# A SwiGLU trunk in float32 halves: seven products of halves moved from the down to the up projection

## The chip, the cores and the metric

The kernel runs on one core of one Trainium2 chip. The metric is the device time of one execution in microseconds; the time before is the median of three runs, 2036.55 us (2036.38 to 2037.76).

## The reference

Two layers over a sequence of 512 tokens of width 1024, in float32. Each layer is SwiGLU, mixer (mLSTM in the first, sparse attention "NSA" in the second), SwiGLU; between the layers a shared K/V set is made. The four SwiGLUs are what the change rewrites:

```python
def rmsnorm(x, g):
    y = xf * lax.rsqrt(jnp.mean(xf * xf, axis=-1, keepdims=True) + EPS)
    return (y * g.astype(jnp.float32)).astype(x.dtype)

def swiglu(h, w_in, w_out):                 # w_in: 1024 x 5632, w_out: 2816 x 1024
    a, b = jnp.split(h @ w_in, 2, axis=-1)
    return (jax.nn.silu(a) * b) @ w_out
...
        h = h + 0.5 * swiglu(rmsnorm(h, ffn_norm[layer, 0]), ffn_w_in[layer, 0], ffn_w_out[layer, 0])
```

## The kernel before, in words

The stages run in the order ffn0, mLSTM, ffn1, K/V, ffn2, NSA, ffn3. The stream `h` lies transposed: eight tiles of 128 features x 512 tokens. A float32 product is made of three passes: each operand is split into a high part (rounded, written by ACT) and a low part (the rest, written by DVE), and `mm3` issues high x high, high x low and low x high. So one "strip" (a 128x128 block of weights times a 128x512 block of the stream) is three matmuls on PE, each with its own weight load (PEld).

A SwiGLU (`ffn`) goes through its 22 column blocks of 128 in pieces (`EVENS`: 8, 8, 6). For each block p it makes the gate block (columns p) and the up block (columns 22 + p), 8 strips each; DVE multiplies both by the row of 1/rms (`r`), ACT applies silu, DVE multiplies them and the result is split. After each piece the down projection adds to `h`: four pairs of output blocks, each 2n strips for a piece of n blocks.

In ffn 0, 1 and 3 (`SEVEN`) some pairs of down blocks (`PAIRS`, five of twelve) are made by Strassen's seven products of a 2x2 product instead of eight: the weights of the pair are quartered (`fetch`: q11, q12, q21, q22), DVE makes four sums of them (`add_quarters`: s1 to s4), the seven resulting forms are split like weights (`load_forms`, four groups: two, two, two and one form), and the gated values are halved along the tokens, with their own three sums (`gate_forms`). `down_seven` then runs seven products of 128x256 (`product`), into the halves of four PSUM banks X, Y, Z, V, and combines them on ACT and DVE.

Weights are loaded by `load_weight` in the order in which they are asked for; `weight` keeps two entries ready beyond the one in use, in three buffers of high and low parts (`whi`, `wlo`, 1024 columns: one whole block of weights, or one group of forms). The entry two ahead can so be split only when PE is done with the one before the current. Every engine works its own instructions in a fixed order, which the compiler's scheduler sets.

Of the kernel before, what the change touches and what calls it, by code (L numbers as in the profile page):

```python
# [96 lines left out]
class Net:  # L97
# [76 lines left out]
    def add_quarters(self, i, m, k0, n):

        q = self.raws[i, m, k0]
        s = self.sums[i, m, k0] = [None] + [self.fp.tile([P, 512], F32, name=f"s{j}", tag=f"s{j}", bufs=1)[:, :n * P]
                                            for j in range(1, 5)]
        self.nc.vector.tensor_tensor(s[1], q[2, 1], q[2, 2], op=ALU.add)
        self.nc.vector.tensor_tensor(s[3], q[1, 1], q[2, 1], op=ALU.subtract)  # L180
        self.nc.vector.tensor_tensor(s[2], s[1], q[1, 1], op=ALU.subtract)
        self.nc.vector.tensor_tensor(s[4], q[1, 2], s[2], op=ALU.subtract)

    def load_forms(self, i, m, k0, n, group):

        q, s = self.raws[i, m, k0], self.sums[i, m, k0]
        forms = ((q[1, 1], s[2]), (s[1], s[3]), (s[4], q[1, 2]), (q[2, 2],))[group]
# [3 lines left out]
        for j, f in enumerate(forms):  # L191
            c = slice(512 * j, 512 * j + n * P)
# [35 lines left out]
    def setup(self):  # L228
# [7 lines left out]
        for b in range(KB):  # L236
# [5 lines left out]
            if b == 1 and self.order:  # L242
                self.load_weight()
# [11 lines left out]
    def norm_in(self, gcol, ssq=True, loaded=False):  # L255
# [82 lines left out]
    def ffn(self, i, r=None):  # L338
# [4 lines left out]
        with ExitStack() as ctx:  # L343
# [23 lines left out]
            def gate_forms(pa, pb):  # L367


                fl = lambda t: t.rearrange("p f n -> p (f n)")  # L370
                if not half:
                    t = gp.tile([P, 3 * N], F32, name="ft", tag="ft", bufs=2)
                    gated(t[:, :T], pa, pb)
                    TT(t[:, T:], t[:, :N], t[:, N:T], op=ALU.subtract)
                    hi = gp.tile([P, 8, N], F32R, name="fhi", tag="fhi", bufs=4)
                    lo = gp.tile([P, 8, N], F32R, name="flo", tag="flo", bufs=4)
                    self.split(t, fl(hi[:, :3]), fl(lo[:, :3]))
                    gs.append((hi, lo))
                    half.append(t)
                    return  # L380
                one, (hi, lo) = half.pop(), gs[-1]
                t = gp.tile([P, 5 * N], F32, name="fv", tag="fv", bufs=1)
                gated(t[:, :T], pa, pb)
                self.split(t[:, :T], fl(hi[:, 3:5]), fl(lo[:, 3:5]))
                c = [t[:, N * j:N * j + N] for j in range(5)]
# [71 lines left out]
            for k0, k1 in EVENS if seven else THIRDS:  # L457
                gs, late, half = [], [], []
                n = k1 - k0
                for p in range(k0, k1):  # L460
# [3 lines left out]
                    if p == 0:  # L464
                        order.sort(key=lambda o: o[0] + 1.5 * o[1])
# [859 lines left out]
```

## Time and profile before

| | before |
|---|---|
| median of 3 runs | 2036.55 us |
| the profiled execution, own time | 2037.12 us |
| its span, first to last instruction | 2035.3 us |
| PE busy | 2020.1 us, 99% |
| DVE busy | 1298.4 us, 64% |
| ACT busy | 885.7 us, 44% |
| granted TensorE clock, mean | 1.000 |

The span is the time from the first to the last instruction of the profiled execution; its own time has 1.8 us more around it. PE's busy time overlaps from one matmul to the next (a record of 0.39 us, starts 0.23 us apart), so what a matmul costs is the distance between two starts. The same holds for DVE, whose records overlap by some 0.08 us.

### The profile page before, as it was taken

To read this page: it belongs to the slowest core of one execution; us is meant where nothing else is said; L and a number is where in the kernel's file an instruction comes from. 1 tells how busy PE (TensorE), PEld (TensorE's weight loads), DVE (VectorE), ACT (ScalarE), POOL (GpSimd) and SP (SyncE) were. 2 spreads that over 40 slices of the span, in tenths; PEclk is the share of its full clock that TensorE was granted. 3 is DMA by queue.
4 is the path that set the end of the run, shared out by engine and by line. 5 is a ranking of instruction groups with operands and counts; after the bars stand their busy time and mean duration, and the time that the engine had idled before them with its cause. 6 is when DMAs were issued, how large, how long until landed. Compare 5 with 4: busy or idle time off the path is not lost.

```text
span 2035.3 us, 26085 instructions
## 1 busy us (share of the span) xinstructions
PE 2020.1 (99%) x10007; PEld 1677.1 (82%) x10007; DVE 1298.4 (64%) x2192; ACT 885.7 (44%) x1533; POOL 163.7 (8%) x216
## 2 busy tenths in 40 slices
PE   9999999999999999999999999999999999999999
PEld 7888888788778888888888888888777788888887
DVE  7565656767786655657656444445778885565654
ACT  5333334445743333334443322224889863333332
POOL 0000000012200000000101000001444410000000
PEclk9999999999999999999999999999999999999999
DMA  5333322323223333322333333323111123233232
GB/s 189 98 99 94 95 91 68 117 83 94 63 99 103 89 108 94 88 94 88 99 116 115 115 93 93 104 89 102 52 43 43 42 80 102 78 118 94 74 111 80
DMA packets 61084, 188.22 MB, mean 92 GB/s; under 512 B 7328, under 2 KB 9760, under 8 KB 60960
## 3 DMA queue, kind: packets, MB, share of 16 engines
q1 hardware_dynamic: 59568, 183.82, 29.3%
q8 instruction: 78, 1.28, 0.3%
q10 hardware_dynamic: 1008, 1.70, 0.2%
q0 software_dynamic: 384, 1.05, 0.2%
q14 instruction: 46, 0.38, 0.1%
HBM read 177.10 MB, written 2.10 MB: 88 GB/s over the span
## 4 chain that ended last, share of the span: by engine, by line
PE 92%; DVE 3%; ACT 3%; DMA 1%; issue 1%; POOL 0%; SPq 0%; DVEq 0%; ACTq 0%
PE pmm L215 82%; PE S L215 3%; PE po L215 2%; PE vps L215 1%; PE pt L1094 1%; PE paux L215 1%; ACT pr L1062 1%; PE pn L215 1%; DVE wlo L158 1%; ACT whi L157 0%; ACT pth L224 0%; PE pt L215 0%; PE dm L215 0%; DMA q<-in_ffn_out 0%; DMA wraw<-in_ffn_in 0%
## 5 line engine op out<-in xcount | busy, mean ns | idle before, releaser
L215 PE MATMUL pmm<-xhi,whi 128*128 128x512 f32 x1672 | 656.6, 393 | 0.7 <-ACT whi L157 0.5
L215 PE MATMUL pmm<-xhi,wlo 128*128 128x512 f32 x1672 | 652.8, 391 | 0.2
L215 PE MATMUL pmm<-xlo,whi 128*128 128x512 f32 x1672 | 652.3, 390 | 0.6 <-DVE xlo L268 0.6
L157 ACT ACTIVATE whi<-wraw 128x1024 fp32r<-128x1024 f32 (+5 forms) x368 | 329.7, 908 | 640.7 <-PE pmm L215 510.8
L158 DVE TENSOR_TENSOR wlo<-wraw,whi 128x1024 fp32r<-128x1024 f32 (+5 forms) x368 | 386.0, 1057 | 75.2 <-ACT whi L157 73.0
L215 PEld LDWEIGHTS pmm<-xhi,wlo 128*128 128x128 f32 x1672 | 313.4, 187 | 66.7 <-DVE wlo L158 1.1
L215 PEld LDWEIGHTS pmm<-xhi,whi 128*128 128x128 f32 x1672 | 313.7, 188 | 63.6 <-ACT whi L157 1.0
L215 PEld LDWEIGHTS pmm<-xlo,whi 128*128 128x128 f32 x1672 | 313.6, 188 | 62.7 <-DVE xlo L268 1.4
L215 PE MATMUL pmm<-fhi,whi 128*128 128x256 f32 (+1 forms) x699 | 230.9, 330 | 0.0
L215 PE MATMUL pmm<-flo,whi 128*128 128x256 f32 (+1 forms) x699 | 229.0, 329 | 0.0
L215 PE MATMUL pmm<-fhi,wlo 128*128 128x256 f32 (+1 forms) x699 | 228.8, 328 | 0.0
L356 DVE TENSOR_TENSOR fu<-pmm,r 128x512 f32<-128x512 f32 x88 | 60.8, 691 | 252.3 <-PE pmm L215 252.3
L215 PEld LDWEIGHTS pmm<-fhi,whi 128*128 128x128 f32 x699 | 132.7, 190 | 14.8 <-ACT fw L435 2.8
L215 PEld LDWEIGHTS pmm<-flo,whi 128*128 128x128 f32 x699 | 132.7, 190 | 11.9
L215 PEld LDWEIGHTS pmm<-fhi,wlo 128*128 128x128 f32 x699 | 132.6, 190 | 11.8
L415 DVE SCALAR_TENSOR_TENSOR h<-pmm,h 128x512 f32<-128x512 f32 (+1 forms) x67 | 45.5, 682 | 116.4 <-PE pmm L215 116.4
L278 POOL TENSOR_TENSOR ssq<-ssq,sq 128x512 f32<-128x512 f32 x18 | 26.5, 1470 | 1038.2 <-ACT sq L277 1006.0
L1067 POOL TENSOR_SCALAR pr<-pr,rz,gate 128x512 f32<-128x512 f32 (+3 forms) x128 | 81.8, 645 | 108.7 <-DVE rz L1063 92.9
L224 ACT ACTIVATE fhi<-fv 128x512 fp32r<-128x512 f32 x66 | 48.8, 740 | 84.2 <-DVE fv L388 61.0
L1062 ACT ACTIVATE pr<-S,nx,c 128x512 f32<-128x512 f32 (+3 forms) x128 | 78.1, 615 | 6.7 <-PE pt L1094 5.6
L354 DVE TENSOR_TENSOR ft<-pmm,r 128x512 f32<-128x512 f32 x55 | 37.9, 688 | 57.2 <-PE pmm L215 50.9
L224 ACT ACTIVATE whi<-s 128x512 fp32r<-128x512 f32 (+1 forms) x60 | 33.8, 601 | 89.9 <-PE pmm L215 63.7
(341 smaller groups left out, 2762.2 us busy)
## 6 DMA issues: line engine op xcount, KB each, us to landing
wraw<-in_ffn_in SPq DMA_DIRECT2D x175, 512.0 KB, 3.5
wraw<-in_ffn_out SPq DMA_DIRECT2D x32, 512.0 KB, 3.6
q<-in_ffn_out SPq DMA_DIRECT2D x48, 256.0 KB, 2.8
wraw<-in_ffn_out SPq DMA_DIRECT2D x16, 448.0 KB, 3.3
wraw<-in_ffn_out SPq DMA_DIRECT2D x18, 384.0 KB, 3.2
wraw<-in_m_qk SPq DMA_DIRECT2D x8, 512.0 KB, 3.5
wraw<-in_m_v SPq DMA_DIRECT2D x8, 512.0 KB, 3.6
wraw<-in_m_og SPq DMA_DIRECT2D x8, 512.0 KB, 3.5
```

The lines of the kernel that those rows point to most:

```text
L157: nc.scalar.activation(hi[:p, c], raw[:p, c], AF.Copy)
L158: nc.vector.tensor_tensor(lo[:p, c], raw[:p, c], hi[:p, c].bitcast(F32), op=ALU.subtract)
L215: self.nc.tensor.matmul(out, lhsT, rhs, start=start, stop=stop)
L224: self.nc.scalar.activation(hi, src, AF.Copy)
L278: (nc.gpsimd if b < 4 else nc.vector).tensor_tensor(t, t, sq, op=ALU.add)
L354: TT(t, pa, r, op=ALU.mult)
L356: TT(u, pb, r, op=ALU.mult)
L415: STT(h[:, c], po[j][:, c], 0.5, h[:, c], op0=ALU.mult, op1=ALU.add)
L1062: nc.scalar.activation(s, S[:, i, :n], AF.Exp, bias=nx[:, i:i + 1], scale=cc, accum_out=z[:, i:i + 1])
L1067: nc.gpsimd.tensor_scalar(s, s, rz[:, i:i + 1], gate[:, tb, gi:gi + 1], op0=ALU.mult, op1=ALU.mult)
L1094: nc.tensor.transpose(pt[:, col:col + P], pr[br][:, ROW[tb] + sb * P:ROW[tb] + sb * P + P], self.ident)
```

## The change

In ffn 0, 1 and 3 no down block is made by seven products any more. Instead, `by_seven` makes pairs of up blocks by seven products of halves: all pairs but the first (blocks 0 and 1), ten a SwiGLU. For the pairs 4, 10, 14 and 20 (`GATES`) the gate blocks are made that way too, four more. Here the 2x2 cut is over two column blocks, the two halves of the 1024 input features and the two halves of the tokens. The forms of the stream are made once a SwiGLU, behind `norm_in` (`x_forms`: four sums of each pair of stream tiles, split into `thi` and `tlo`), while the two plain pairs of the first two blocks run. A raw quarter has two buffers (before one).

The up value is not multiplied by 1/rms any more, in all four SwiGLUs; `gate_plain` takes it straight from PSUM. The factor goes onto the down result: instead of one DVE instruction (h += 0.5 * po) there are two (d = 0.5 * po * r; h += d). The first block's strips are ordered with the up block 3.5 strips behind the gate block (before 1.5), and the second weight of the kernel is fetched after four of the eight tiles of x (before after two). In the mLSTM, `sigmoids` (a table load and four activations on ACT) is called inside `finish`, behind its Square, instead of ahead of `finish`.

```diff
-PAIRS = {0: (1, 3), 8: (1, 3), 16: (1,)}
+GATES = (4, 10, 14, 20)
...
+            def x_forms(k):
+                one, two = (gp.tile([P, 3 * N], F32, name="fw", tag="fw", bufs=2) for _ in range(2))
+                h2, c = self.h[k + 4], [two[:, N * j:N * j + N] for j in range(3)]
+                nc.scalar.activation(one[:, :T], self.h[k], AF.Copy, scale=g1)
+                TT(one[:, T:], one[:, N:T], one[:, :N], op=ALU.subtract)
+                STT(c[0], h2[:, N:], g2, one[:, T:], op0=ALU.mult, op1=ALU.subtract)
+                STT(c[1], h2[:, N:], g2, one[:, N:T], op0=ALU.mult, op1=ALU.subtract)
+                STT(c[2], h2[:, :N], g2, c[0], op0=ALU.mult, op1=ALU.subtract)
...
+                self.split(one[:, T:], hi[:, :N], lo[:, :N])
+                self.split(two, hi[:, N:], lo[:, N:])
...
+            def by_seven(p):
...
+                upcoming("fetch", p)
+                a11, s1 = self.weight("form", i, p, 0)
+                yield from product(X[:, :N], a11, 0)
+                nc.scalar.activation(W[:, 0, :], X[:, :N], AF.Copy)
+                yield from product(Y[:, :N], s1, -1)
+                s2, s3 = self.weight("form", i, p, 1)
+                yield from product(X[:, N:], s2, -2)
+                TT(U, X[:, N:], W[:, 0, :], op=ALU.add)
+                yield from product(Y[:, N:], s3, -3)
+                TT(W[:, 1:, :], U[:, None, :].to_broadcast([P, 2, N]), two(Y), op=ALU.add)
+                TT(u2[:, N:], W[:, 2, :], Y[:, :N], op=ALU.add)
+                s4, a12 = self.weight("form", i, p, 2)
+                yield from product(Z[:, N:], s4, 3)
+                yield from product(Z[:, :N], a12, 2)
+                TT(two(u1), W[:, :2, :], two(Z), op=ALU.add)
+                a22 = self.weight("form", i, p, 3)[0]
+                upcoming("add", p)
+                yield from product(V[:, :N], a22, -4)
+                TT(u2[:, :N], W[:, 2, :], V[:, :N], op=ALU.add)
+                return u1, u2
...
-                        STT(h[:, c], po[j][:, c], 0.5, h[:, c], op0=ALU.mult, op1=ALU.add)
...
+                            STT(d[:, c], po[j][:, c], 0.5, r[:, c], op0=ALU.mult, op1=ALU.mult)
+                            TT(h[:, c], h[:, c], d[:, c], op=ALU.add)
...
                 nc.scalar.activation(dc, pt[:, :, :H], AF.Square)
+
+                sigmoids(half)
...
             weave(heads(1), rest, 1.0)
-            sigmoids(1)
             weave(finish(1), rest, 5)
```

Three places of the order in which the engines work. First PE, where a unit of seven products begins. Before, in the first pair of down blocks by seven (`pmm_889` is its bank X, `pmm_890` its bank Y, `whi_825` holds the forms a11 and s2, `whi_831` s1 and s3):

```order
L215 MATMUL pmm_889<-flo_731,whi_825 128x256
L215 MATMUL pmm_889<-fhi_730,wlo_826 128x256
L215 MATMUL pmm_890<-fhi_348,whi_831 128x256
L215 MATMUL pmm_890<-flo_349,whi_831 128x256
L215 MATMUL pmm_890<-fhi_348,wlo_832 128x256
L215 MATMUL pmm_890<-fhi_434,whi_831 128x256
L215 MATMUL pmm_889<-fhi_348,whi_825 128x256
L215 MATMUL pmm_889<-flo_349,whi_825 128x256
```

Four matmuls into Y, then back into X, the first half of which ACT has to copy out. Now, in the first pair of up blocks (`pmm_501` is X, `pmm_502` is Y; twelve matmuls into Y in all, of which the first three are shown, and behind them X again):

```order
L213 MATMUL pmm_501<-xlo_150,whi_433 128x256
L213 MATMUL pmm_501<-xhi_149,wlo_434 128x256
L213 MATMUL pmm_502<-thi_352,whi_433 128x256
L213 MATMUL pmm_502<-tlo_353,whi_433 128x256
L213 MATMUL pmm_502<-thi_352,wlo_434 128x256
...
L213 MATMUL pmm_501<-thi_352,whi_467 128x256
L213 MATMUL pmm_501<-tlo_353,whi_467 128x256
```

The return to X moved from four matmuls behind its first half to twelve.

Second DVE, inside a unit of seven products. Before, in that pair of down blocks (`fq`, `fw`, `fr` are its combinations, `wlo` low parts of weights or forms, `s_` sums for the next such pair):

```order
L438 TENSOR_TENSOR fq_894<-pmm_889,fw_893 128x256
L225 TENSOR_TENSOR wlo_929<-q22_815,whi_928 128x512
L443 TENSOR_TENSOR fw_893<-fq_894,pmm_890 128x2x256
L444 TENSOR_TENSOR fr_895<-fw_893,pmm_890 128x256
L158 TENSOR_TENSOR wlo_961<-wraw_958,whi_960 128x1024
L179 TENSOR_TENSOR s1_1018<-q21_1014,q22_1016 128x512
L449 TENSOR_TENSOR fw_893<-fw_893,pmm_891 128x512
```

Now, in the gate unit of pair 4 of ffn 0 (the sums are those of its up unit, `wlo_734` and `wlo_765` that unit's first two groups of forms):

```order
L410 TENSOR_TENSOR fq_652<-pmm_647,fw_651 128x256
L178 TENSOR_TENSOR s2_718<-s1_717,q11_579 128x512
L413 TENSOR_TENSOR fw_651<-fq_652,pmm_648 128x512
L179 TENSOR_TENSOR s3_719<-q11_579,q21_583 128x512
L415 TENSOR_TENSOR fu_654<-fw_651,pmm_648 128x256
L180 TENSOR_TENSOR s4_720<-q12_581,s2_718 128x512
L223 TENSOR_TENSOR wlo_734<-q11_579,whi_733 128x512
L223 TENSOR_TENSOR wlo_734<-s1_717,whi_733 128x512
L420 TENSOR_TENSOR fu_653<-fw_651,pmm_649 128x512
L223 TENSOR_TENSOR wlo_765<-s2_718,whi_764 128x512
```

Where plain weights and sums with a plain pair in between stood, sums and forms of the unit that comes next now stand back to back.

Third ACT, at the end of the mLSTM. Before (`th` is a split of the last head, `ds` the sums that `finish` starts from, `dc` its Square):

```order
L224 ACTIVATE th_4708<-sqn_4699 128x512
L765 ACT_TABLE_LOAD
L765 ACTIVATE sig_4347<-sig_4347 128x512
L765 ACTIVATE sig_4442<-sig_4442 128x512
L765 ACTIVATE sig_4507<-sig_4507 128x512
L765 ACTIVATE sig_4602<-sig_4602 128x512
L708 COPY ds_4728<-dm_4260 40x512
L157 ACTIVATE whi_4774<-wraw_4772 128x512 x2
L714 ACTIVATE dc_4735<-pnm_4730 128x32
```

Now:

```order
L222 ACTIVATE th_5400<-sqn_5391 128x512
L730 COPY ds_5416<-dm_4952 40x512
L736 ACTIVATE dc_5423<-pnm_5418 128x32
L789 ACT_TABLE_LOAD
L789 ACTIVATE sig_5039<-sig_5039 128x512
L789 ACTIVATE sig_5134<-sig_5134 128x512
L789 ACTIVATE sig_5199<-sig_5199 128x512
L789 ACTIVATE sig_5294<-sig_5294 128x512
L157 ACTIVATE whi_5466<-wraw_5464 128x512 x2
```

The table load and the four sigmoids moved behind the copy and the Square, ahead of the next weights.

## Rows read from the trace of the kernel before

**Rows 1.** The page: its first line, and busy time, share of the span and instructions of each engine.

```profile
span 2035.3 us, 26085 instructions
...
PE 2020.1 (99%) x10007; PEld 1677.1 (82%) x10007; DVE 1298.4 (64%) x2192; ACT 885.7 (44%) x1533; POOL 163.7 (8%) x216
```

**Rows 2.** The page: the chain of work that ended last, its shares of the span by engine.

```profile
PE 92%; DVE 3%; ACT 3%; DMA 1%; issue 1%; POOL 0%; SPq 0%; DVEq 0%; ACTq 0%
```

**Rows 3.** Busy time by stretch (start:end in us, its length, then busy time of PE, PEld, DVE, ACT, POOL with instruction counts, the granted clock, DMA share, GB/s): the first SwiGLU before and after its first 10.3 us, and most of the second (ffn 1).

```profile
0.00:10.30 10.30, 7.84 (x35) 5.83 (x35) 4.50 (x9) 6.75 (x11) 1.48 (x5) 1.00 0.78 291
10.30:367.00 356.70, 356.70 (x1763) 302.81 (x1764) 229.60 (x337) 134.55 (x182) 7.97 (x8) 1.00 0.32 100
592.50:963.00 370.50, 370.49 (x1828) 314.53 (x1829) 232.84 (x344) 138.61 (x186) 4.40 (x3) 1.00 0.30 94
```

**Rows 4.** The chain that ended last, in order of time (start, us, what): one piece of it, PE alone, in the SwiGLU that has no products of halves.

```profile
1144.96 269.39 PE pmm L215 x1188
```

**Rows 5.** Instructions of PE in order of time (start us, us, engine line op out<-in): the end of a product of halves, and the first matmul behind it.

```profile
118.07 0.28 PE L215 MATMUL pmm<-fhi,wlo 128*128 128x256 f32 x1
118.19 0.28 PE L215 MATMUL pmm<-fhi,whi 128*128 128x256 f32 x1
118.31 0.28 PE L215 MATMUL pmm<-flo,whi 128*128 128x256 f32 x1
118.43 0.28 PE L215 MATMUL pmm<-fhi,wlo 128*128 128x256 f32 x1
118.55 0.40 PE L215 MATMUL pmm<-fhi,whi 128*128 128x512 f32 x1
```

**Rows 6.** Busy time by stretch, columns as in rows 3: one pair of down blocks by seven products with four row blocks a half (84 matmuls, the other stretch of the kind is the same), and one with three (63).

```profile
108.23:118.55 10.32, 10.32 (x85) 10.11 (x84) 9.02 (x16) 4.68 (x7) 0.00 (x0) 1.00 0.26 62
...
342.74:350.52 7.78, 7.78 (x64) 7.59 (x63) 7.63 (x14) 5.76 (x11) 1.30 (x1) 1.00 0.00 0
```

**Rows 7.** PE inside the first of these, in order of time; and who weight loads waited for over the whole span (us in total, times, longest).

```profile
110.03 0.66 PE L215 MATMUL pmm<-fhi,whi 128*128 128x256 f32 x2
110.52 0.28 PE L215 MATMUL pmm<-flo,whi 128*128 128x256 f32 x1
...
PEld pmm L215 <- ACT fw L435: 2.8, 14, 0.2
```

**Rows 8.** Instructions of DVE in order of time, in the same pair of down blocks.

```profile
117.92 0.69 DVE L181 TENSOR_TENSOR s<-s,q 128x512 f32<-128x512 f32 x1
118.52 0.69 DVE L450 SCALAR_TENSOR_TENSOR h<-fw,h 128x512 f32<-128x512 f32 x1
119.12 1.22 DVE L158 TENSOR_TENSOR wlo<-wraw,whi 128x1024 fp32r<-128x1024 f32 x1
120.26 0.42 DVE L454 TENSOR_TENSOR fr<-fw,pmm 128x256 f32<-128x256 f32 x1
120.59 0.69 DVE L182 TENSOR_TENSOR s<-q,s 128x512 f32<-128x512 f32 x1
121.19 0.69 DVE L455 SCALAR_TENSOR_TENSOR h<-fr,h 128x512 f32<-128x512 f32 x1
```

**Rows 9.** Groups of DVE and ACT instructions of one shape (count | busy us, mean ns of one | idle time before them and what ended it).

```profile
L158 DVE TENSOR_TENSOR wlo<-wraw,whi 128x1024 fp32r<-128x1024 f32 x223 | 274.4, 1231 | 39.0 <-ACT whi L157 38.5
...
L225 DVE TENSOR_TENSOR wlo<-s,whi 128x512 fp32r<-128x512 f32 x48 | 31.9, 686 | 0.2
...
L225 DVE TENSOR_TENSOR flo<-fv,fhi 128x768 fp32r<-128x768 f32 x33 | 31.6, 958 | 27.4 <-ACT fhi L224 27.4
L224 ACT ACTIVATE whi<-s 128x512 fp32r<-128x512 f32 x48 | 28.2, 622 | 82.1 <-PE pmm L215 55.9 <-issue 26.2
```

**Rows 10.** The start of ffn 1, in order of time: three rows of DVE, one of PE.

```profile
585.94 1.79 DVE L268 SCALAR_TENSOR_TENSOR xlo<-h,gains,xhi 128x512 fp32r<-128x512 f32 x1
...
602.77 0.69 DVE L290 TENSOR_TENSOR ssq<-ssq,ssq 128x512 f32<-128x512 f32 x1
608.66 2.59 DVE L158 TENSOR_TENSOR wlo<-wraw,whi 128x1024 fp32r<-128x1024 f32 x2 [5.20 <-ACT whi L157]
...
592.51 0.47 PE L215 MATMUL pmm<-yhi,whi 128*128 128x512 f32 x1 [1.08 <-DVE h L746]
```

**Rows 11.** The end of the mLSTM, ACT in order of time: the second call of `sigmoids` and what is behind it; and the stretch behind that, columns as in rows 3.

```profile
554.84 1.28 ACT L765 ACT_TABLE_LOAD   x1
556.13 2.19 ACT L765 ACTIVATE sig<-sig 128x512 f32<-128x512 f32 x4
558.23 0.56 ACT L708 COPY ds<-dm 40x512 f32<-40x512 f32 x1
...
559.75 0.18 ACT L714 ACTIVATE dc<-pnm 128x32 f32<-128x32 f32 x1
...
563.00:592.60 29.60, 27.31 (x114) 19.77 (x113) 25.84 (x43) 12.48 (x21) 4.15 (x3) 1.00 0.36 115
```

**Rows 12.** The last instructions of the kernel, in order of time.

```profile
2031.12 0.39 PE L215 MATMUL pmm<-fhi,wlo 128*128 128x512 f32 x1
2031.54 0.76 DVE L415 SCALAR_TENSOR_TENSOR h<-pmm,h 128x256 f32<-128x256 f32 x2 [3.39 <-PE pmm L215]
...
2032.33 0.34 ACTq L1203 DMA_DIRECT2D out_dram<-h  x1
```

**Rows 13.** DMA issues (line, engine, count, KB each, median us to landing).

```profile
q<-in_ffn_out SPq DMA_DIRECT2D x48, 256.0 KB, 2.8
```

More of the change, by code (lines that the diff above doesn't have):

```diff
@@ L241, in setup @@
                     self.load_first()
-            if b == 1 and self.order:
+            if b == 3 and self.order:
                 self.load_weight()
@@ L281, in norm_in @@
             parts(b)
-            if loaded and b == 1:
+            if loaded and b == 2:
                 self.rest()
@@ L365, in gate @@
                 gs.append((hi, lo))
[L367 to L385, printed above, removed]
-                TT(c[2], c[0], one[:, T:], op=ALU.subtract)
-                TT(c[3], c[0], one[:, :N], op=ALU.subtract)
-                TT(c[4], c[1], c[2], op=ALU.subtract)
-                self.split(t[:, T:], fl(hi[:, 5:]), fl(lo[:, 5:]))
@@ L429, in down_seven @@
+            def by_seven(p):
+                X, Y, Z, V = (ps_mm() for _ in range(4))
                 two = lambda t: t.rearrange("p (c n) -> p c n", n=N)
                 W = gp.tile([P, 3, N], F32, name="fw", tag="fw", bufs=2)
-                u2 = gp.tile([P, N], F32, name="fq", tag="fq", bufs=1)
-                q = gp.tile([P, T], F32, name="fr", tag="fr", bufs=1)
-                a11, s2 = self.weight("form", *at, 0)
-                yield from product(X[:, :N], a11, 1)
-                nc.scalar.activation(W[:, 1, :], X[:, :N], AF.Copy)
@@ new lines, in by_seven, with strip, plain @@
+                return u1, u2
+            def strip(ps, w, k):
+                self.mm3(ps, self.strip(w, k), x[k], k == 0, k == KB - 1)
+            def plain(p):
+                if p == 1:
+                    upcoming("fetch", None)
+                w2 = [self.weight("ffn_in", i, p + j * FB) for j in range(2)]
+                if p == 1:
+                    upcoming("add", None)
+                ps = ps_mm(), ps_mm()
+                order = [(k, j) for j in range(2) for k in range(KB)]
+                if p == 0:
+                    order.sort(key=lambda o: o[0] + 3.5 * o[1])
+                for t, (k, j) in enumerate(order):
+                    if p == 1 and t == 3 and r is None:
+                        columns.append(self.rstd_columns(ssq, ps_mm())[0])
+                    if p == 1 and t == KB + 4 and r is None:
+                        rows.append(self.rstd_rows(columns[0], ps_mm()))
+                    if seven and p == 1 and t >= 12:
+                        x_forms(t - 12)
+                    strip(ps[j], w2[j], k)
+                    yield
+                late.append(ps)
@@ L769, in mlstm @@
             run(rest)
-            sigmoids(0)
             weave(project_v(1), finish(0), 0.25)
@@ L1286, in layout @@
     d["ffn_in"] = np.stack([blocks(w) for w in wi])
-    mated = np.concatenate([np.r_[a:b:2, a + 1:b:2] for a, b in EVENS])
-    d["ffn_out"] = np.stack([blocks(w)[:, :, mated if j in SEVEN else slice(None)] for j, w in enumerate(wo)])
+    d["ffn_out"] = np.stack([blocks(w) for w in wo])
     w = f["a_w_in"][0]
```

174 lines of the change are left out of this document (80 added, 94 removed).

## The prediction

> **What bounds the kernel now.** The page comes first: PE is busy 99% of the span, DVE 64%, ACT 44% [rows 1], and the chain of work that ended last lies on PE for 92% [rows 2]. So a change is worth what it takes off PE, as long as no other engine makes PE wait. The stretches say the same for the SwiGLUs alone: from 10.3 us to 367 us PE has no idle time at all, and DVE 229.6 us of records in 356.7 [rows 3].
>
> A busy PE is not a price, so the price of a matmul is the distance between starts. A plain one (128x512) costs 269.39 / 1188 = 0.2268 us [rows 4]. One of half the columns costs 0.12 us [rows 5], more than half of 0.2268 (0.1134): in the stretch of such products the weight loads are busy 10.11 of 10.32 us [rows 6], so 0.12 is what a weight load takes, and I let it stand for the new ones, which load the same 128x128 tiles.
>
> On DVE too the starts count: 128x512 instructions start 0.60 us apart, one of 1024 takes 1.14 us and one of 256 0.33 us until the next [rows 8], though the records say 0.69, 1.22 and 0.42.
>
> **The products.** A pair of blocks over eight strips is 48 plain matmuls, 48 x 0.2268 = 10.89 us. By seven products it is 84 of half width, 84 x 0.12 = 10.08 us. The old units took 10.32 us [rows 6], 0.24 more: in the middle of the unit two matmuls take 0.49 us, not 0.24 [rows 7], and weight loads waited 14 times, 0.2 us at most, for ACT's copy of the first half of X. Matmuls into X come back there after only four into Y. In the new order twelve lie between, 1.44 us, and the copy, of 256 columns, is shorter than a high part of 512, 0.62 us [rows 9], so the gap should go.
>
> The five old units of a SwiGLU saved 4 x (10.89 - 10.32) + (36 x 0.2268 - 7.78) = 2.28 + 0.38 = 2.66 us [rows 4, 6]. The fourteen new ones save 14 x (10.89 - 10.08) = 11.3 us. Three SwiGLUs: 3 x (11.3 - 2.66) = 25.9 us less PE time. If the gap stays in each new unit, 42 x 0.24 = 10.1 us of it goes again.
>
> **What DVE has to do for it.** A unit of seven products costs DVE seven low parts and four sums of 512 columns (11 x 0.60 = 6.6 us) and five combinations (three of 256, two of 512: 2.2 us), 8.8 us in all. The gate of a pair is six instructions of 512, 3.6 us. A pair with plain gate blocks is then 2 x 1.14 + 8.8 + 3.6 = 14.7 us of DVE against 10.89 + 10.08 = 20.97 us of PE, 6.3 us to spare. A pair by halves on both sides (4, 10, 14, 20) is 2 x 8.8 + 3.6 = 21.2 us of DVE against 20.16 us of PE: DVE is 1.08 us behind. Unpaid, that is 12 x 1.08 = 13 us. By the records, 0.69 us, a unit would be 11 x 0.69 + 2.6 = 10.2 us and such a pair 2 x 10.2 + 6 x 0.69 = 24.5 us, 4.4 too many; I take the distances, because they hold where sums, updates and low parts follow each other [rows 8].
>
> [...]
>
> Of the 13 us I take nothing. In front of each such pair stands one with 6.3 us to spare, behind it another or the down blocks, and forms are made two groups ahead. I walked DVE's new order through pairs 2, 4 and 6 by these distances, an ACT high part at 0.6 us [rows 9], time zero at the up unit of pair 2. The sums of the next unit fill DVE's waits. The first forms of pair 4's up unit are ready at 18.8 us where PE wants them at 20.2; the first plain weights of pair 6 at 29.5 us, wanted at 30.2. At the down blocks behind pair 14 the second weight comes 0.4 us before it is wanted. These margins (1.4, 0.7, 0.4 us) are thin, and that is where I expect an error. ACT has 14 high parts, four gate activations and two copies in such a pair, some 12 of 20 us. A quarter lands 2.8 us after its issue [rows 13]; the tightest, q22 of the unit after next, leaves DVE about 0.7 us in that walk.
>
> The forms of the stream cost DVE, for each of four pairs of tiles, four instructions of 256 (0.33 to 0.40), one low part of 256 and one of 768 (0.96 [rows 9], about 0.87 to the next): 2.75 us, 11 us a SwiGLU. They are wanted only after the plain blocks 0 and 1 and the gate blocks of pair 2, some 34 us after PE starts, and DVE has holes there: in ffn 1 it has nothing to do from 603.5 us to 608.7 [rows 10]. I count 35 us of DVE work up to the last form, beginning a microsecond before PE does, and take nothing; a late last form would cost what it is late, a microsecond or two a SwiGLU. But a few pieces stand ahead of the updates of h at the end of the mLSTM's output projection. There DVE is late already: PE waited 1.08 us for an update of h, and a low part of x took 1.79 us [rows 10]. Two or three instructions of 0.34 more: +1.0 us (0 to +3).
>
> **The small parts.** Dropping u * r takes 0.60 us of DVE per block, and the second instruction on a down result adds 0.60 per output block; both lie beside PE, whose down blocks take 10.89 us a pair where DVE needs 2 x 1.14 + 4 x 0.60 = 4.7. Only at the very end is it on the path: the last h is two instructions [rows 12] and becomes four, 2 x 0.34 = +0.7 us. `sigmoids`: the table load and four sigmoids occupy ACT from 554.84 us to 558.2, ahead of the copy from which `finish` starts, and the Square comes at 559.75 [rows 11]. Behind the Square they lie beside the chain of 1/rms on DVE, which so starts about 3.5 us earlier. What that can give is the idle time of PE behind it, 29.60 - 27.31 = 2.3 us [rows 11], part of it for the updates of h: -1.5 (0 to -2.3). The order at the start: PE idles 2.5 us of its first 10.3 [rows 3], part of it before its first instruction; -0.5 (0 to -1.4).
>
> **The sum.** -25.9 - 1.5 - 0.5 + 0.7 + 1.0 = -26.2 us. Against the profiled execution's own time, 2037.12, that gives 2010.9 us; the median of the runs is 0.57 us below that execution, so 2010.4, rounded 2010.5 us.
>
> **The rivals.**
>
> *The debt of the four pairs is paid each time.* If the head start isn't there when such a pair begins (a high part late on ACT, a quarter late, margins of 0.4 us eaten by hand-overs between engines), all 13 us come back: 2023.5 us. For it: the thin margins, and that DVE is the fullest engine beside PE. Against: the spare 6.3 us ahead of every such pair.
>
> *The gap on X stays.* 42 x 0.24 us: 2020.5 us. Against it is the order of PE; for it, that ACT's copy stands in a queue behind high parts whose buffers PE must free.
>
> *DVE becomes the bound.* If DVE's instructions cost what their records last, because each waits for the one before or for ACT, twelve pairs lose 12 x 4.4 = 52 us: 2062.5 us, slower. It decides from 22.3 us of DVE per such pair on (12 x 2.2 us = 26), which is 0.63 us an instruction instead of 0.60, with no head start carried over. Against it: the starts 0.60 us apart [rows 8]; for it, that the new order has sums which need the sum just before them, and low parts whose high parts ACT writes in the same moment.
>
> *Nothing is won.* If the first group of every new unit comes 0.62 us late, 42 x 0.62 = 26 us are lost and the time is 2036.5 us. Nothing in the old units, with the same buffers, points to it: PE idles in none.
>
> **How the numbers follow.** Forecast (2005 to 2016): 0.60. Debt paid wholly or mostly (2016 to 2030): 0.20. Gap stays: 0.09. DVE the bound, slower: 0.07. Nothing won: 0.04. The median of three runs moves by less than 0.1%, so 0.2% (4.1 us) is taken as the least that can be told from no change. Faster 0.89, same 0.04, slower 0.07. The likeliest time is 2010.5 us. The range goes down to 2005 (all small terms at their better ends give 2007.6, and 2.6 us for the distances, which are read to 0.01 us) and up to 2024, the debt paid in full.
>
> **What would show it.** After: 3528 records of half width with starts 0.12 us apart; a new unit 10.1 us long with no wait for the copy of X; each of the three SwiGLUs about 8.6 us shorter (ffn 0 about 348 us from its first steady matmul); DVE busy near 1450 us (one SwiGLU up from about 229 to 281 us of records); the end of the chain 0.7 us longer. Wrong if, in pairs 4, 10, 14 and 20, PE or its weight loads wait for low parts (`wlo` from `q` or `s`, or the first `ffn_out` weights), or in the first up unit for `tlo`.

## The result

| | before | after |
|---|---|---|
| median of the runs timed together (4 each) | 2036.47 us | 2020.22 us (2018.68 to 2021.05) |
| ratio after to before | | 0.9918, 95% interval 0.9901 to 0.9935 |
| the profiled execution, own time / span | 2037.12 / 2035.3 us | 2020.29 / 2018.1 us |
| PE / DVE / ACT busy | [rows 1] | 1999.6 / 1422.4 / 926.7 us |
| granted TensorE clock, mean | 1.000 | 0.998 |

Faster by 0.8%, inside the range, but 9.7 us above the 2010.5 that was forecast, and outside the band of 2005 to 2016 that had most of the chances. By the time alone it would pass for the rival in which the gap on X stays (2020.5 us); the trace has to tell them apart. The page of the changed kernel, its span and its busy times:

```profile
span 2018.1 us, 28665 instructions
...
PE 1999.6 (99%) x11006; PEld 1709.9 (85%) x11006; DVE 1422.4 (70%) x2486; ACT 926.7 (46%) x1698; POOL 165.5 (8%) x216
```

To see where the 9.7 us are, I cut both executions at the same matmuls (first of the mLSTM's gates `pg`, last of its output projection, first `paux` of K/V, last of NSA's output projection, last of all), each at its start. us per stretch; `last_one`, `forms_behind` and `both` are experiments told below:

| stretch | before | after | change | forecast | last_one | forms_behind | both |
|---|---|---|---|---|---|---|---|
| start and ffn 0 | 366.88 | 361.81 | -5.1 | -9.1 | 363.04 | 360.82 | 360.89 |
| mLSTM | 230.97 | 229.15 | -1.8 | -0.5 | 229.00 | 228.16 | 227.77 |
| ffn 1, first strips of K/V | 364.10 | 358.22 | -5.9 | -8.6 | 355.62 | 357.58 | 355.60 |
| K/V, ffn 2, NSA | 710.96 | 713.04 | +2.1 | 0 | 710.41 | 711.81 | 710.13 |
| ffn 3 | 358.21 | 351.39 | -6.8 | -8.6 | 351.40 | 349.97 | 349.93 |
| behind the last matmul | 4.22 | 4.53 | +0.3 | +0.7 | 3.85 | 4.52 | 3.87 |

The products themselves came as forecast. Windows of the changed kernel (columns as in rows 3): one up unit, and the stretch of pair 10 (the up unit of pair 8, then gate and up unit of pair 10), to be held against the old unit of 10.32 us [rows 6]:

```profile
86.61:96.69 10.08, 10.08 (x82) 9.93 (x81) 6.21 (x10) 4.15 (x7) 0.00 (x0) 1.00 0.21 72
193.27:223.50 30.23, 30.23 (x253) 30.23 (x252) 27.95 (x49) 15.79 (x27) 0.00 (x0) 1.00 0.28 88
```

10.08 us, and 30.23 for three. 17 of the 18 stretches of half-width matmuls are like that (10.07 or 10.08 us a unit); in the first of all PE waited once, 0.65 us, for ACT's copy (`fw L405`). Weight loads waited for that copy 14 times before [rows 7], now once:

```profile
PEld pmm L213 <- ACT fw L405: 0.7, 1, 0.7
```

So, that one wait apart, neither the gap on X nor the debt of the four pairs took anything inside the units. What is missing stands at the seams. First the start of K/V, PE in order of time; before, PE had no such wait there:

```profile
945.67 0.39 PE L213 MATMUL pmm<-xhi,wlo 128*128 128x512 f32 x1
947.00 0.51 PE L213 MATMUL pmm<-xhi,whi 128*128 128x512 f32 x1 [0.94 <-ACT xhi L265]
947.78 0.50 PE L213 MATMUL pmm<-xlo,whi 128*128 128x512 f32 x1 [0.28 <-DVE xlo L266]
...
949.18 1.86 PE L213 MATMUL paux<-ones,ssq 128*128 128x1 f32 x8 [0.67 <-DVE ssq L288]
950.91 0.77 PE L213 MATMUL pmm<-xhi,whi 128*128 128x512 f32 x1
951.48 0.63 PE L213 MATMUL pmm<-xlo,whi 128*128 128x512 f32 x1
951.91 0.63 PE L213 MATMUL pmm<-xhi,wlo 128*128 128x512 f32 x1
```

The last tile of x is late: 1.33 us between two starts instead of 0.23, then 0.78 and 1.06, 2.5 us lost in all. And behind it the starts are 0.43 us apart, because the granted clock fell to its half (windows as in rows 3):

```profile
945.00:950.00 5.00, 3.11 (x12) 1.86 (x11) 3.84 (x6) 2.40 (x4) 0.00 (x0) 0.92 0.36 105
950.00:955.00 5.00, 5.00 (x15) 4.13 (x16) 2.97 (x14) 0.00 (x0) 0.00 (x0) 0.50 0.26 66
955.00:960.00 5.00, 5.00 (x26) 4.22 (x25) 0.45 (x1) 1.11 (x3) 0.00 (x0) 0.90 0.11 43
```

Some twelve matmuls at 0.43 us instead of 0.23, 2.4 us, lie in the next stretch of the table, which is 2.1 us longer.

Second the starts of the SwiGLUs: the chain of 1/rms stands on DVE among the forms of the stream. DVE at the start of ffn 3, and PE behind it:

```profile
1677.38 0.95 DVE L223 TENSOR_TENSOR tlo<-fw,thi 128x768 fp32r<-128x768 f32 x1
1678.37 0.48 DVE L375 SCALAR_TENSOR_TENSOR fw<-h,gains,fw 128x256 f32<-128x256 f32 x1
1678.77 1.22 DVE L158 TENSOR_TENSOR wlo<-wraw,whi 128x1024 fp32r<-128x1024 f32 x1
1679.90 0.15 DVE L309 TENSOR_SCALAR rv<-pmm 128x4 f32<-128x4 f32 x1
1679.97 0.47 DVE L376 SCALAR_TENSOR_TENSOR fw<-h,gains,fw 128x256 f32<-128x256 f32 x1
1680.37 0.16 DVE L297 TENSOR_SCALAR rq<-rv 128x4 int32<-128x4 int32 x1
...
1683.55 0.16 DVE L302 SCALAR_TENSOR_TENSOR rc<-rq,rc 128x4 f32<-128x4 f32 x1
...
1683.77 1.16 PE L213 MATMUL pmm<-cst,rc 128*128 128x128 f32 x8 [1.17 <-DVE rc L302]
```

In ffn 0 the same chain ran from 24.06 to 31.16 us, and PE waited for it at 31.21.

### The profile page after: what moved, and what is told of

It reads as the page before. It is cut to its first block, busy times and chain, and to the rows that moved or that the text cites. A ratio compares the mean times of both kernels' runs of the same rounds, so it can differ in the third digit from the quotient of the medians.

```text
span 2018.1 us, 28665 instructions
## 1 busy us (share of the span) xinstructions
PE 1999.6 (99%) x11006; PEld 1709.9 (85%) x11006; DVE 1422.4 (70%) x2486; ACT 926.7 (46%) x1698; POOL 165.5 (8%) x216
## 3 DMA queue, kind: packets, MB, share of 16 engines
q0 software_dynamic: 384, 1.05, 0.2%
## 4 chain that ended last, share of the span: by engine, by line
PE 87%; DVE 6%; ACT 3%; issue 1%; DMA 1%; POOL 0%; DVEq 0%; ACTq 0%
PE pmm L213 76%; PE S L213 3%; PE po L213 2%; PE vps L213 1%; PE pt L1116 1%; DVE wlo L158 1%; PE paux L213 1%; ACT pr L1084 1%; PE pn L213 1%; ACT whi L157 0%; DVE xlo L266 0%; PE pt L213 0%; ACT pth L222 0%; PE dm L213 0%; ACT xhi L265 0%
## 5 line engine op out<-in xcount | busy, mean ns | idle before, releaser
L213 PE MATMUL pmm<-xhi,whi 128*128 128x512 f32 (+1 forms) x1504 | 538.7, 358 | 1.3 <-ACT xhi L265 0.9
L213 PE MATMUL pmm<-xlo,whi 128*128 128x512 f32 (+1 forms) x1504 | 534.8, 356 | 0.8 <-DVE xlo L266 0.8
L213 PE MATMUL pmm<-xhi,wlo 128*128 128x512 f32 (+1 forms) x1504 | 534.7, 356 | 0.9 <-DVE wlo L158 0.9
L157 ACT ACTIVATE whi<-wraw 128x1024 fp32r<-128x1024 f32 (+6 forms) x314 | 269.9, 876 | 573.9 <-PE pmm L213 461.0
L158 DVE TENSOR_TENSOR wlo<-wraw,whi 128x1024 fp32r<-128x1024 f32 (+6 forms) x314 | 320.4, 1030 | 57.7 <-ACT whi L157 55.6
L213 PE MATMUL pmm<-ghi,whi 128*128 128x512 f32 x704 | 274.2, 389 | 0.0
L213 PE MATMUL pmm<-glo,whi 128*128 128x512 f32 x704 | 274.0, 389 | 0.0
L213 PE MATMUL pmm<-ghi,wlo 128*128 128x512 f32 x704 | 273.7, 389 | 0.0
L213 PE MATMUL pmm<-thi,whi 128*128 128x256 f32 x672 | 190.3, 283 | 0.5 <-ACT fw L405 0.5
L213 PE MATMUL pmm<-tlo,whi 128*128 128x256 f32 x672 | 190.2, 283 | 0.0
```

The lines of the kernel that those rows point to most:

```text
L157: nc.scalar.activation(hi[:p, c], raw[:p, c], AF.Copy)
L158: nc.vector.tensor_tensor(lo[:p, c], raw[:p, c], hi[:p, c].bitcast(F32), op=ALU.subtract)
L213: self.nc.tensor.matmul(out, lhsT, rhs, start=start, stop=stop)
```

## The experiments

Each time stands beside 2036.3 to 2037.2 us for the kernel before on the same chip; the ratios to it have intervals of 0.0013 to 0.0016 either side. All but `before_again` are edits of the changed kernel.

**last_one: one instruction for each update of h in the last piece.**

```diff
+                if early:
+                    TT(t, t, r, op=ALU.mult)
                 TT(t, t, u, op=ALU.mult)
...
+                            gate(t, u, k0 == 16)
...
+                            if seven and k0 == 16:
+                                STT(h[:, c], po[j][:, c], 0.5, h[:, c], op0=ALU.mult, op1=ALU.add)
+                                continue
```

> In the last of the three pieces of ffn 0, 1 and 3 the factor 1/rms is put back on the gated value (one more DVE instruction of 128x512 for each of six blocks, 0.60 us each) and the update of h is one DVE instruction again; all else as in the changed kernel (2020.2 us). Theory: the second instruction of the update, and the low parts of weights that stand between the two, make the wait at the start of K/V (2.6 us in three pieces) and with it the fall of the granted clock behind it (about 2.5 us). Then no wait of PE over 0.3 us at the start of K/V, granted clock 1.00 behind it, the end of the kernel 0.3 us shorter: about 2014.8 us (2013.5 to 2016.5). Rival: the wait goes and the clock falls all the same, 2017.3. Rival: the wait comes from DVE being behind since the pair 20, made by halves on both sides; then six more instructions there make it longer, 2020 to 2023.

2014.16 us (2013.88 to 2015.1), 6.1 less. K/V starts without a wait, clock 1.000, and the two stretches there are 2.6 us shorter each. (By the table ffn 0 is 1.2 us longer in its profile.) Why two instructions were too many shows in DVE's order of time in the last down blocks of ffn 1. The changed kernel:

```profile
923.43 0.96 DVE L158 TENSOR_TENSOR wlo<-wraw,whi 128x768 fp32r<-128x768 f32 x1 [1.00 <-ACT whi L157]
...
927.54 0.68 DVE L502 SCALAR_TENSOR_TENSOR fd<-pmm,r 128x512 f32<-128x512 f32 x1
928.14 1.47 DVE L158 TENSOR_TENSOR wlo<-wraw,whi 128x768 fp32r<-128x768 f32 x1
929.54 0.68 DVE L503 TENSOR_TENSOR h<-h,fd 128x512 f32<-128x512 f32 x1
931.01 0.75 DVE L266 SCALAR_TENSOR_TENSOR xlo<-h,gains,xhi 128x512 fp32r<-128x512 f32 x1 [0.79 <-ACT xhi L265]
931.67 0.68 DVE L502 SCALAR_TENSOR_TENSOR fd<-pmm,r 128x512 f32<-128x512 f32 x1
```

and `last_one`:

```profile
924.55 0.96 DVE L158 TENSOR_TENSOR wlo<-wraw,whi 128x768 fp32r<-128x768 f32 x1 [1.84 <-ACT whi L157]
...
930.17 0.69 DVE L504 SCALAR_TENSOR_TENSOR h<-pmm,h 128x512 f32<-128x512 f32 x1 [1.36 <-PE pmm L213]
930.83 0.96 DVE L158 TENSOR_TENSOR wlo<-wraw,whi 128x768 fp32r<-128x768 f32 x1
931.71 0.74 DVE L266 SCALAR_TENSOR_TENSOR xlo<-h,gains,xhi 128x512 fp32r<-128x512 f32 x1
934.25 0.69 DVE L504 SCALAR_TENSOR_TENSOR h<-pmm,h 128x512 f32<-128x512 f32 x1 [1.80 <-PE pmm L213]
```

In both a weight lands late, and ACT, and behind it DVE, wait for it. ACT in the changed kernel, in `last_one` and in `forms_behind` (told next), one row of each:

```profile
922.55 0.85 ACT L157 ACTIVATE whi<-wraw 128x768 fp32r<-128x768 f32 x1 [1.28 <-DMA wraw<-in_ffn_out]
923.67 0.85 ACT L157 ACTIVATE whi<-wraw 128x768 fp32r<-128x768 f32 x1 [2.74 <-DMA wraw<-in_ffn_out]
919.92 0.85 ACT L157 ACTIVATE whi<-wraw 128x768 fp32r<-128x768 f32 x1 [0.66 <-DMA wraw<-in_ffn_out]
```

With two instructions the ring of one output block (`fd`, low part, `h`, ACT's `xhi`, `xlo`, next `fd`) takes 931.67 - 927.54 = 4.13 us, and PE makes an output block in 18 x 0.2268 = 4.08: what is lost once is never made up and comes out at K/V. With one instruction DVE waits for PE again two blocks later, though its delay was the longer one.

The other profiles with two instructions bear this out: the distance between two starts ahead of the late tile of x follows ACT's wait for that weight. It is 1.33 us for a wait of 1.28 in the changed kernel, 1.11 for 1.07 in `sig_back`, 1.10 for 1.05 in `old_start` and 0.71 for 0.66 in `forms_behind`; where no such wait stands (`gates_none`, `x_gap`, `gates_all`) the tile comes in time. So the ring keeps a delay and does not make it. Why the weight lands late in some kernels and not in others is not shown.

**forms_behind: the forms of the stream behind the chain of 1/rms on DVE.**

```diff
-            STT(out, t, 1.5, out, op0=ALU.add, op1=ALU.mult)
+            self.chain = STT(out, t, 1.5, out, op0=ALU.add, op1=ALU.mult)
...
-                        x_forms(t - 12)
+                        with tc.issue_after(self.chain.ins):
+                            x_forms(t - 12)
```

> The changed kernel with the forms of x put on DVE behind the last instruction of the 1/rms chain (issue order only); nothing else changed. Theory: the pieces of the forms inside and ahead of that chain make PE wait for it (1.0 us in ffn 0, 1.7 in ffn 3): both waits go, the chain from rv to rc lasts under 3 us in ffn 0 instead of 6.9, 2017.6 us (2016.5 to 2018.5). Rival: the forms, started later, are now late for the first unit of seven products, and what was won is lost there: 2019.5 to 2023, with PE or its weight loads waiting for tlo or for the first form weights. Rival: the chain was late because of the squares and the weights ahead of it: 2020.2, the waits stay.

2014.59 us (2013.71 to 2015.68), 5.6 less, twice what was expected. The waits for `rc` are gone; the chain of ffn 0 now begins and ends at

```profile
23.89 0.15 DVE L309 TENSOR_SCALAR rv<-pmm 128x4 f32<-128x4 f32 x1
...
26.06 0.16 DVE L302 SCALAR_TENSOR_TENSOR rc<-rq,rc 128x4 f32<-128x4 f32 x1
```

2.3 us instead of 7.1. By stretches: ffn 0 1.0, ffn 3 1.4, and three that I had not counted. The end of the mLSTM is 1.0 shorter: the last wait for an update of h there (in the changed kernel PE starts 1.15 us late at 585.64) is gone, so the forms did stand ahead of the updates. The stretch of ffn 1 is 0.6 shorter, not at its start but at its end, where the late weight of `last_one` lands 0.6 us less late (1.28 and 0.66 above). And the fall of the clock at K/V was shorter, eight matmuls instead of twelve (1.2). These last two, some 1.8 of the 5.6 us, come with that transfer and not with the chain; that the order of the forms moved it is not shown. No wait of PE is put down to `thi` or `tlo`; the first unit of ffn 0 waited 0.44 us for a low part of its weights.

**both: the two edits together.**

> last_one and forms_behind together: in the last piece of ffn 0, 1 and 3 the factor 1/rms on the gated value and one instruction for each update of h; the forms of x behind the 1/rms chain on DVE. Theory: the two are different losses (the start of K/V, and the starts of the SwiGLUs), which share only some 1 us behind the wait at K/V: 2020.2 - 6.1 - 5.6 + 1.2 = 2009.7 us (2008 to 2011.5), no wait of PE over 0.3 us at the start of K/V, none for rc, the clock at 1.00 throughout. That would be the time forecast for the change, so the two steps would be all that the forecast missed. Rival: both act through the same wait or the same fall of the clock: 2014.

2010.10 us (2008.98 to 2010.81), ratio 0.9868 (0.9852 to 0.9884), clock 1.000. The two losses add up, and with them out of the way the kernel has the time forecast for the change. Not by every term, though: ffn 0 stays 3.1 us short of its forecast and the mLSTM is 2.7 better, so that the total meets the forecast is in part luck.

**factor_back: the factor on the gate in all pieces of ffn 0, 1 and 3.** The edit is that of `last_one` without its condition, for the plain blocks 0 and 1 too.

> The changed kernel with the factor 1/rms back on the gated values of all pieces of ffn 0, 1 and 3 (one more DVE instruction of 128x512 per block) and each update of h one instruction. A pair by halves on both sides then takes DVE 22.4 us by the distances, 2.24 more than PE. Theory: the head start (2.8 us, from gates_all, where the third pair in a row waits 0.41 at a debt of 3.2) covers a single such pair, so moving the factor was worth nothing to PE in the pairs, and only the wait at K/V counts: 2014.2 us, as last_one (2013 to 2016). Rival: the margins are spent, and each of twelve pairs pays 1 us or more: 2024 and above, with PE waiting for wlo in pairs 4, 10, 14 and 20.

2015.32 us (2015.12 to 2016.93). One pair waited, pair 4 of ffn 0 (1.51 us for `wlo` at 68.71); in the other eleven the stretch of three units is 30.23 or 30.24 us. So the room on DVE that moving the factor bought was needed once, for 1.5 us, and the kernel without the move is 4.9 us faster.

**gates_none: all gate blocks plain.** `GATES = ()`.

> The changed kernel with all gate blocks plain (no pair by halves on both sides). Theory: the twelve gate units each gave their full 10.89 - 10.08 = 0.81 us, none of it lost to DVE's debt: 2020.2 + 9.7 = 2029.9 us (2028 to 2031). Rival: the debt was paid somewhere that the units do not show (later waits, the start of K/V): 2020 to 2026.

2025.71 us (2025.44 to 2026.31), 5.5 more instead of 9.7, in the rival's range. DVE's order at K/V is the same, but there no weight lands late in the last down blocks, PE waits 0.58 us instead of 2.5, and the clock stays at 1.00. Of the 9.7 us that the twelve gate units save, 4.2 went there. Against `last_one`, which has no such loss, the difference is 11.5 us; 0.6 of it is the wait left at K/V and 1.3 the time behind the last matmul (5.17 us against 3.85), so the units do give their 9.7.

**gates_all: ten pairs by halves on both sides.** `GATES = (2, 4, ..., 20)`.

> The changed kernel with the gate blocks of all ten pairs (2 to 20) made by seven products, 18 more units in all. By PE alone each saves 10.89 - 10.08 = 0.81 us: 2020.2 - 14.6 = 2005.6. By my distances between starts on DVE (0.60 us) each of the ten pairs of a SwiGLU leaves DVE 1.08 us behind, 10.8 a SwiGLU, of which some 1 us a piece is covered: +2.9 us a SwiGLU on balance, about 2029 us (2021 to 2038), PE waiting for forms in the later pairs of each piece. If DVE's instructions cost what their records last (0.69 us), each pair is 4.4 us too long: 3 x (44 - 3 - 5) = +108, near 2128 us.

2020.12 us (2018.61 to 2021.14): no change, just below the range expected. PE in the middle piece of ffn 0 (pairs 8 to 14), the rows with a wait:

```profile
197.44 0.39 PE L213 MATMUL pmm<-xhi,wlo 128*128 128x256 f32 x1 [0.25 <-DVE wlo L223]
218.67 0.39 PE L213 MATMUL pmm<-xhi,wlo 128*128 128x256 f32 x1 [0.83 <-DVE wlo L223]
```

Two such pairs in a row wait for nothing there, the third's up unit starts 0.41 us late, the fourth's 0.98. (In the first piece of ffn 0, where DVE comes from the forms of x, it is the second and the third.) Over the three SwiGLUs these waits come to 7.6 us. Behind down blocks DVE's head start is thus worth more than two debts of 1.08, and distances of 0.60 are the right price: by record lengths each pair would have lost 4.4. The piece was 82.21 us for eight units of 10.08, DVE busy for 79.67 of them. More of what 18 units should have brought went to pair 2 of ffn 0, which waited 2.8 us for the first form of x, and to waits for `rc`, 3.3 us in ffn 3 and 1.0 in ffn 1. Behind the two longest of these waits the granted clock was 0.50 for 3.4 us each.

**both_gates8: `both` with `GATES = (4, 6, 8, 10, 12, 16, 18, 20)`.**

> The kernel both, with the gate blocks of eight pairs (4, 6, 8, 10, 12, 16, 18, 20) made by seven products, four more a SwiGLU. In gates_all the third such pair in a row made PE wait 0.41 us, the fourth 0.98, the first two nothing, and pair 2 waited for the forms of x; so 12 x 0.81 = 9.7 us less of PE, 3 x 2 x 0.41 = 2.5 us of waits: 2009.7 - 7.2 = 2002.5 us (2000.5 to 2005). Rival: the factor on the gate in the last piece (3.6 us of DVE more) eats the head start there, and pairs 18 and 20 wait 2 us each: about 2011. If every pair paid the 1.08 us that the distances give: 2009.7 - 9.7 + 24 x 1.08 = 2026.

2012.98 us (2011.34 to 2013.36), slower than `both`: the rival came. With the factor on the gate in the last piece its third pair in a row waits 1.84 us (2.13 in ffn 3, and behind that the granted clock was 0.50 for 3.4 us), pairs 6 and 12 0.41 or more, and the h update at the start of ffn 1 is late again (1.29). A gate unit saves 0.81, so with that factor a third pair in a row is a loss.

**x_gap: the old order of the first products.**

```diff
-        forms = ((q[1, 1], s[1]), (s[2], s[3]), (s[4], q[1, 2]), (q[2, 2],))[group]
+        forms = ((q[1, 1], s[2]), (s[1], s[3]), (s[4], q[1, 2]), (q[2, 2],))[group]
...
-                a11, s1 = self.weight("form", i, p, 0)
+                a11, s2 = self.weight("form", i, p, 0)
                 yield from product(X[:, :N], a11, 0)
...
-                yield from product(Y[:, :N], s1, -1)
-                s2, s3 = self.weight("form", i, p, 1)
                 yield from product(X[:, N:], s2, -2)
...
+                s1, s3 = self.weight("form", i, p, 1)
+                yield from product(Y[:, :N], s1, -1)
```

> The changed kernel with the order of the first products of a unit as in the old units: both halves of X from the first group of forms, then Y; PE then returns to X after six matmuls into Y instead of twelve (before the change after four, with 0.24 us of waiting). Theory: the wait is for ACT's copy of the first half; in the old units the return came 5 x 0.12 + 0.24 = 0.84 us behind the start of the last matmul into the first half, and seven starts of 0.12 are 0.84 too, so a gap of 0 to 0.1 us stays in each unit: 2020 to 2024.5, units of 10.08 to 10.2 us. Rival: the gap belongs to the return to the bank itself and not to the copy: 42 x 0.24, 2030, units of 10.32.

2026.71 us (2026.49 to 2027.98), above the range, units of 10.32 to 10.34 us, the length that the rival gave. The six matmuls in my expectation were those of the first unit alone; in the other 41 the program puts four into Y, as before the change. Who weight loads waited for; and the copy and the waiting load in the first unit of ffn 1, in order of time:

```profile
PEld pmm L213 <- ACT fw L405: 9.9, 42, 1.4
```

```profile
631.80 0.38 ACT L405 ACTIVATE fw<-pmm 128x256 f32<-128x256 f32 x1
...
632.24 0.19 PEld L213 LDWEIGHTS pmm<-thi,whi 128*128 128x128 f32 x1 [0.20 <-ACT fw L405]
```

42 waits, one in each unit, and the load begins when the copy has ended (632.18). Against the rival, a return to the bank that costs by itself, speaks the one wait of the changed kernel, in its first unit: there twelve matmuls lie between, but the copy is late, and PE's load waits for its end (49.10) all the same:

```profile
48.73 0.37 ACT L405 ACTIVATE fw<-pmm 128x256 f32<-128x256 f32 x1
...
49.14 0.19 PEld L213 LDWEIGHTS pmm<-thi,whi 128*128 128x128 f32 x1 [0.69 <-ACT fw L405]
```

The gap was the copy, and the twelve matmuls removed it: 42 x 0.25 = 10.5 us. The whole is only 6.5 us slower because K/V loses less here: PE waits 0.58 us for the last square, as in `gates_none`, and the clock stays at 1.00.

**old_start: the three edits at the start undone.**

```diff
-            if b == 3 and self.order:
+            if b == 1 and self.order:
...
-            if loaded and b == 2:
+            if loaded and b == 1:
...
-                    order.sort(key=lambda o: o[0] + 3.5 * o[1])
+                    order.sort(key=lambda o: o[0] + 1.5 * o[1])
```

> The changed kernel with the three edits at its start undone: second weight fetched after two tiles of x, the rest of the first weight split after two, up block 1.5 strips behind the gate block. Theory: these edits are what puts the first matmul of a block at 7.07 us (5.72 before), and of the 3.4 us by which the first 52 us lost more on PE, about 0.9 are theirs (the other 2.5 are waits behind the forms of x): 2019.3 us (2018.3 to 2020.2), first matmul near 5.7, idle time of PE in the first 52 us near 9 instead of 10. Rival: all 3.4 us are theirs, since a later start also shifts what DVE does next: 2016.8, idle 6.6. Rival: none, 2020.2.

2024.17 us (2020.41 to 2025.46), 4 more, but not as any theory had it. The profiled run (2020.41, clock 0.999) starts its blocks at 7.04 us as well; PE idles 1.0 us for a low part ahead of 22.56, and behind that the clock falls (windows as in rows 3):

```profile
20.00:24.00 4.00, 2.70 (x15) 2.17 (x15) 4.00 (x6) 1.36 (x2) 0.00 (x0) 0.98 0.14 22
24.00:28.00 4.00, 4.00 (x13) 3.14 (x12) 3.55 (x15) 1.37 (x2) 0.00 (x0) 0.59 0.80 270
```

Three of its five runs had a mean clock of 0.997 and 2024 to 2025 us, two 0.999 and 2020.4 to 2020.8. Whether the three edits keep the clock up, four runs of the changed kernel against five do not settle, and where it fell in the slower ones no profile shows.

**sig_back: the sigmoids ahead of `finish` again.**

> The changed kernel with the sigmoids of the mLSTM called ahead of finish again, as before the change. By the forecast's term the end of the mLSTM gets 1.5 us longer: 2021.7 us (2020.5 to 2022.5), the idle time of PE at its end near 2.3 us again. By the sums of the stretches (mLSTM 1.8 us shorter after the change, 2.8 with the forms of x out of the way) the move is worth 2 to 2.8: 2022.2 to 2023. Rival: the sigmoids were hidden anyway: 2020.2.

2021.38 us (2020.5 to 2023.58), 1.2 more, with ranges that overlap (2018.68 to 2021.05 with the move). In the two profiles the mLSTM differs by 2.0 us (231.16 against 229.15).

**before_again: the kernel before, once more.**

> The kernel before, once more, for its start: theory, the first matmul of a block stands at 5.7 us as in the first profile, and the 6.1 to 7.1 us of all kernels with the change are the change's; rival, it is when the first transfers land, which differs from run to run by a microsecond: anywhere from 5.7 to 7.1 here too. About 2036.5 us either way.

2038.26 us. Its first block starts at 6.61 us, not 5.72: that moment differs from run to run. What PE loses in the first 52 us (52 us less its matmuls at 0.2268 and 0.12) is 6.6 us in both runs of before, 10.0 in the changed kernel and 8.9 to 9.0 with the forms behind the chain. Among kernels with the same start it is not steady either: 10.2 in `gates_none`, 10.7 in `sig_back`, 11.3 in `last_one`.

**best: the free places alone.** `forms_behind`; the edit of `last_one` in ffn 1 only; `GATES` 4, 8, 10, 14, 16, 18 (ffn 1: 4, 8, 10, 14, 18).

> The forms of x behind the 1/rms chain (as forms_behind); factor 1/rms on the gate and one instruction for each update of h in the last piece of ffn 1 alone; gate blocks by halves in the pairs that gates_all and both_gates8 show free: 4, 8, 10, 14, 16, 18 (ffn 1: 4, 8, 10, 14, 18), never three in a row. Theory: two in a row behind the down blocks wait for nothing, so five more units than both by 0.81 us: 2010.1 - 4.1 = 2006.0 us (2004.5 to 2008). Rival: the pairs 10 and 18 each pay 0.4 to 1.8 us, as the third in a row did: 2009 to 2013.

2008.81 us (2007.98 to 2009.65), ratio 0.9865 (0.9849 to 0.9881). No pair by halves on both sides waits: four units in a row take 40.32 us. Of 4.1 us expected, 1.6 in ffn 0 and 1.6 in ffn 3 came; 0.84 went to an update of h at the start of ffn 1 that is late again, and 1.0 to the end of the kernel. Beside `both` (0.9868) it is no faster than the intervals allow to say; both beat the changed kernel.

## Why the forecast was right in kind and 9.7 us short

- **The products, -25.9 us: right.** 10.08 us a unit in the trace; `x_gap` shows that the order around X is worth 10.5 of it. With the other losses out of the way (`both`) the stretch of ffn 1 is 8.5 us shorter, where the forecast had 8.6.
- **Nothing for DVE's debt: right.** No pair of the changed kernel waits, `gates_all` pays 0.41 and 0.98 for the third and fourth in a row. DVE's records of 512 columns last 682 ns in the row below, and where none of them waits their starts lie 0.60 us apart (208.79, 209.39 and 209.99 us in the gate unit of pair 10 of ffn 0). As a price the record's length failed, since the rival in which DVE becomes the bound (2062.5 us) did not come. Two figures of the working are off, and nothing rests on them: 21.2 - 20.16 is 1.04 and not 1.08 us, and DVE is busy for 1422.4 us, not near 1450, since records that overlap were added up. DVE's groups of one shape, as in rows 9:

```profile
L223 DVE TENSOR_TENSOR wlo<-s,whi 128x512 fp32r<-128x512 f32 x168 | 111.2, 682 | 0.1
```

- **"Both lie beside PE", the second instruction on a down result: wrong**, and the costliest step. I set DVE's sum, 4.7 us, against PE's 10.89 a pair. But the last piece has six blocks, 8.16 us a pair, and at the end of ffn 1 the splits for K/V stand between: what counts is a ring through DVE and ACT of 4.13 us a block against 4.08 on PE, which has nothing to spare for a transfer that lands late. 2.5 us of waits and 2.6 by the clock (`last_one`); where no weight landed late the same ring cost 0.58 (`gates_none`, `x_gap`).
- **"Take nothing" for the forms: wrong.** I asked only whether the forms come in time for their unit. They did; what they delayed was the chain of 1/rms, which they stood ahead of and among. `forms_behind` gives 5.6 us back: 2.4 of them at the starts of ffn 0 and 3, 1.0 at the end of the mLSTM, some 1.8 at K/V by the earlier transfer. "A microsecond or two a SwiGLU" was named, for the wrong victim.
- **+1.0 for forms ahead of the updates of h: right by its own test** (`forms_behind`, 1.0 us), **-1.5 for the sigmoids: a little small** (`sig_back`, 2.0). The two are not independent, and their sum was off: the mLSTM is 1.8 us shorter where 0.5 was forecast, and with the forms alone (`sig_back`) it is 0.2 longer than before the change (231.16 against 230.97), not 1.0.
- **-0.5 at the start: wrong in sign.** PE loses 3.4 us more in its first 52 us (up to 4.7 in kernels with the same start); 1.0 to 1.1 of that are the forms. The rest, among it three waits of 0.4 to 0.7 us for parts of the first weights and of x, is not settled: undoing the three edits did not remove it.
- **+0.7 at the end: right by its own test, too large as a change.** Among the kernels with the change it is 3.85 to 3.87 us behind the last matmul with one instruction a half, 4.50 to 5.17 with two; but before the change it was 4.22 with one, so +0.3. Where the other 0.4 came from is open.

## What to carry to other kernels

Work that lies beside a busy engine is not free because its sum is smaller: where two other engines hand one block back and forth, compare the round trip with the block's time on the busy engine; where the two are equal (here 4.13 against 4.08 us), a late transfer is kept to the next seam (here the wait of 1.28 us for a weight, and at K/V 1.33 us between two starts). For work that is early enough for its own reader, ask also whose instructions stand behind it in the same queue. And of a unit that fills PE evenly the distances between starts gave the time to 0.1 us; the error of this forecast sat at the seams between stages.

## Not expected of the hardware

The granted clock fell to half its level (0.50) for 6.8 us in the changed kernel (949.2 to 956.0) and for 3.4 us in `old_start`, `forms_behind`, `before_again`, `both_gates8` and, twice, `gates_all`, mostly behind stretches in which PE had waited: at K/V in the changed kernel (busy 3.11 of 5.00 us ahead of it), at the start in `old_start` (2.70 of 4.00). Matmuls of 128x512 then start 0.43 us apart instead of 0.23. Such waits did not always bring it: `old_start` lost 2.3 us at K/V as well, and the clock stayed at 1.00 there. Nor did it take waits of that size: the kernel before, run once more, has a fall in NSA, where PE had been busy for 4.71 of 5.00 us, many of its matmuls of 32 columns (`before_again`, windows as in rows 3):

```profile
1519.00:1524.00 5.00, 4.71 (x33) 4.00 (x31) 3.17 (x8) 3.70 (x11) 1.63 (x3) 1.00 0.15 36
1524.00:1529.00 5.00, 5.00 (x26) 3.76 (x25) 3.46 (x8) 2.38 (x6) 1.36 (x3) 0.66 0.00 0
```

Where the waits at K/V were gone (`last_one`, `both`, `factor_back`), the mean clock of the profiled run was 1.000; three of the changed kernel's four runs have 0.998, and the fourth, with 0.999, is its fastest (2018.68 us). So in the profile of the changed kernel the seam of 2.5 us cost twice that.
